# The last norm of a hybrid attention / recurrence layer: its weights ahead of the root, and several blocks of it in one product

## The chip, the cores and the metric

The kernel runs on one core of a Trainium2 chip. The metric is the device time of one execution, in microseconds (us). Engines: TensorE (PE), its weight loads (PEld), VectorE (DVE), ScalarE (ACT), GpSimd (POOL), and SyncE (SP), which only issues transfers; ScalarE issues some too.

## The reference, cut to what matters

One decoder layer on 1024 tokens of width 1024, all float32. After attention, recurrence and a gated MLP it ends in the MLP's down projection, the residual and a norm:

```python
h = h + conv_glu(u, w_up[layer], conv_w[layer], conv_b[layer], w_down[layer])
return rms_norm(h, final_norm_g)
# rms_norm(x, g) = x * rsqrt(mean(x * x, over the width) + 1e-6) * g
```

## The kernel before

All activations lie transposed: `h_` is a tile of 128 partitions x 8 blocks (`NCT`) x 1024 tokens, where block d holds 128 of the 1024 channels. A sum over the width is thus one over partitions and blocks: the squares of the eight blocks are added up, and a product with a matrix of ones on TensorE (`sum_parts`, L344, or L1377) brings the sum to all partitions.

Most of the down projection runs in seven stages (`STAGES`, L1417 and on; PE lines L1431 to L1433) and is added to `h_` at L1351. The rest, two of the 22 channel groups of the MLP, is done plainly by `down_piece(k, tail)` over `pieces`: piece 0 is tokens 0 to 511, piece 1 tokens 512 to 767, piece 2 tokens 768 to 1023. Pieces 1 and 2 are the end of the program, and the change is there.

- `down_block(d, t, name)`: six products on TensorE for one block (L1362 to L1364, tile `pdl`), and the residual addition on VectorE (L1365: one operand from PSUM, one from SBUF).
- `down_piece`: per block the addition above, a square on ScalarE (`sqf`, L1404; the first into an accumulator directly, `facc`, L1401), and the square's addition to an accumulator (L1405). Piece 1 has two accumulators, added at L1409, and the sum is split into a rounded part and the rest (`facchi` on ScalarE, L338; `facclo` on VectorE, L339) for the product with ones. Piece 2 has four, which go into four products with ones (L1377); its blocks 2 and 4 are added by GpSimd.
- `final(k)`: the product with ones (`ssf`), the root by Ln, Exp and Square on ScalarE (L328 to L330) and two steps on VectorE (`rft` L331, `rfy` L332), and then for each block one VectorE instruction that multiplies h by its weight and by the root (L1384), with a transfer to the output for each two blocks (L1389), or for each one of the last two (L1386).
- `down_piece(2, tail)` gets `final(1)` as `tail` and takes one step of it after each block from d = 4 on, so piece 1's root is worked out beside piece 2's blocks.

TensorE's instructions keep the order in which they are written. Those of the other engines are put in order by a scheduler when the program is built, except where `tc.keep_in_program_order` holds them: held instructions keep the written order among themselves on their engine.

Of the kernel before, what the change touches and what calls it, by code (L numbers as in the profile page):

```python
# [17 lines left out]
P = 128  # L18
SEQ = 1024
DM = 1024  # L20
# [182 lines left out]
def hybrid_kernel(ctx: ExitStack, tc: tile.TileContext, xT, w_qk, w_tok, w_hg, w_out, w_up,  # L203
# [1047 lines left out]
    with pool("ps2", "left", space=PSUM) as ps2:  # L1251
# [117 lines left out]
        facc = {}  # L1369

        def final(k):
            t = pieces[k]
            w = t.stop - t.start
            ss = bank2(f"ssf{k}")
            if k == 2:
                for i in range(4):
                    PE.matmul(ss[:, :w], ones, facc[k][i], start=(i == 0), stop=(i == 3))  # L1377
            else:
                sum_parts(ss[:, :w], facc[k])
            R, tt = (ttile(x, f"rf{x}_{k}", 2) for x in "yt")  # L1380
            rstd_part(R[:, :w], tt[:, :w], ss[:, :w], 1.0 / DM)
            yield
            for d in range(NCT):
                DVE.scalar_tensor_tensor(h_[:, d, t], h_[:, d, t], col(V_GF + d), R[:, :w], op0=ALU.mult, op1=ALU.mult)  # L1384
                if k == 2 and d >= 6:
                    (nc.sync if d % 2 else nc.scalar).dma_start(out[d, :, t], h_[:, d, t])  # L1386
                elif d % 2:
                    q = nc.scalar if k == 2 and d == 3 else nc.sync
                    q.dma_start(out[d - 1 : d + 1, :, t].rearrange("d p t -> p d t"), h_[:, d - 1 : d + 1, t])  # L1389
                yield  # L1390

        def down_piece(k, tail):
            t = pieces[k]
            w = t.stop - t.start
            facc[k] = [None] * 4
            for d in range(NCT):
                down_block(d, t, f"pdl{k}_{d}")
                i = d - 4 if d >= 6 and k == 2 else d % 2
                if facc[k][i] is None:
                    facc[k][i] = ttile(f"acc{i}", f"facc{k}_{i}", 2)[:, :w]  # L1400
                    ACT.activation(facc[k][i], h_[:, d, t], AF.Square)  # L1401
                else:
                    sq = ttile("sq", f"sqf{k}_{d}", 4)[:, :w]
                    ACT.activation(sq, h_[:, d, t], AF.Square)  # L1404
                    (POOL if k == 2 and d % 2 == 0 else DVE).tensor_add(facc[k][i], facc[k][i], sq)  # L1405
                if d >= 4:
                    next(tail, None)
            if k < 2:
                DVE.tensor_add(facc[k][0], facc[k][0], facc[k][1])  # L1409
                facc[k] = parts_of(facc[k][0], lambda x: ttile("sq", f"facc{x}{k}", 4, F32R)[:, :w])  # L1410
            for _ in tail:
                pass

        for x, y in STAGES:
            last = x == "s4"
            if last:
# [5 lines left out]

                down_piece(0, iter(()))
                tail = final(0)
# [36 lines left out]

        down_piece(1, tail)
        tail = final(1)
        down_piece(2, tail)
        for _ in final(2):
            pass
    tp_cm.__exit__(None, None, None)
    down_cm[0].__exit__(None, None, None)
# [64 lines left out]
```

## Time and profile before

| | us |
|---|---|
| median of 3 runs | 1209.05 (1207.75 to 1209.67) |
| the profiled execution | 1207.86 |
| its span, from the first instruction to the last | 1205.9 |
| outside the span | 1.96 |

Busy over the span: PE 1192.7 us (99%), DVE 947.8 (79%), ACT 631.4 (52%), POOL 298.5 (25%). By stretch of the span: from 1183.3 to 1189.0 (piece 1's products) DVE is busy 4.80 of 5.70 us and POOL not at all; from 1189.0 to 1195.4 (piece 2's) DVE 5.62 of 6.40, POOL 1.48; from 1195.4 to 1202.8 DVE 7.29 of 7.40, PE 1.31. Times in the text are microseconds from the start of the span; a bare four-digit time is a point on that clock.

### The profile page before, as it was taken

What the parts mean: (1) busy time and instruction counts of PE and PEld (TensorE: products, weight loads), DVE (VectorE), ACT (ScalarE), POOL (GpSimd) and SP (SyncE); (2) the same over time, 40 slices, a digit from 0 to 9 for tenths busy, and PEclk for the clock granted to TensorE, in tenths of its full rate; (3) what the DMA queues carried; (4) which work ended last, traced back from release to release, by engine and by line L of the source; (5) the groups of instructions that cost most, each with busy time, mean ns of one, the idle gap of its engine ahead of it and who ended that gap; (6) DMA issues with size and microseconds to landing.
All of it is one profiled execution on the core that took longest, in us unless ns stands there. A gap on an engine that the chain in (4) does not pass through costs nothing.

```text
span 1205.9 us, 17474 instructions
## 1 busy us (share of the span) xinstructions
PE 1192.7 (99%) x6014; PEld 1005.6 (83%) x6014; DVE 947.8 (79%) x1783; ACT 631.4 (52%) x1217; POOL 298.5 (25%) x276
## 2 busy tenths in 40 slices
PE   9999999999999999999999999999999999999996
PEld 8988888888888888888888888888888888888886
DVE  8767776666778776484999899898888978957986
ACT  8766666667666565454643343433443444444553
POOL 1154446544001014413231322312223200000000
PEclk9999999999999999999999999999999999999999
DMA  7021112223111123432113323333223267534532
GB/s 273 10 71 54 53 54 88 64 65 120 36 36 54 60 64 112 133 125 94 42 64 114 108 85 106 121 116 109 84 98 122 96 213 249 156 98 158 166 103 89
DMA packets 71833, 122.39 MB, mean 101 GB/s; under 512 B 7360, under 2 KB 17856, under 8 KB 71744
## 3 DMA queue, kind: packets, MB, share of 16 engines
q1 hardware_dynamic: 60528, 101.41, 26.3%
q10 hardware_dynamic: 11216, 19.86, 4.3%
q8 instruction: 47, 0.77, 0.3%
q14 instruction: 42, 0.34, 0.1%
HBM read 97.65 MB, written 23.59 MB: 101 GB/s over the span
## 4 chain that ended last, share of the span: by engine, by line
PE 95%; DVE 3%; ACT 1%; issue 0%; POOL 0%; DVEq 0%; ACTq 0%
PE p L1132 11%; PE p L1133 11%; PE p L1134 11%; PE ds L1433 3%; PE ds L1431 3%; PE ds L1432 3%; PE po L1036 2%; PE po L1038 2%; PE po L1037 2%; PE da L1433 2%; PE da L1431 2%; PE da L1432 2%; PE piv L512 1%; PE piv L514 1%; PE piv L513 1%; PE S L585 1%
## 5 line engine op out<-in xcount | busy, mean ns | idle before, releaser
L88 POOL TENSOR_TENSOR wlo<-raww,whi 128x512 fp32r<-128x512 f32 x141 | 208.6, 1491 | 382.4 <-ACT whi L86 231.6
L86 ACT CAST whi<-raww 128x512 fp32r<-128x512 f32 x276 | 167.7, 617 | 183.9 <-DVE raww L120 69.1
L88 DVE TENSOR_TENSOR wlo<-raww,whi 128x512 fp32r<-128x512 f32 x136 | 97.5, 717 | 22.8 <-ACT whi L86 22.7
L86 ACT CAST whi<-r 128x512 fp32r<-128x512 f32 x70 | 43.6, 623 | 83.1 <-PE ds L1432 51.3
L597 POOL TENSOR_SCALAR P<-P,st 128x512 f32<-128x512 f32 (+2 forms) x96 | 55.8, 592 | 107.9 <-DVE st L594 50.5
L588 DVE CUSTOM_DVE_ANT_0 P<-S,mask 128x512 f32<-128x512 f32 (+2 forms) x96 | 52.0, 553 | 29.9 <-PE S L586 28.9
L593 ACT ACTIVATE P<-P,st 128x128 f32<-128x128 f32 (+3 forms) x64 | 49.7, 777 | 32.0 <-DVE st L588 16.7
L88 DVE TENSOR_TENSOR wlo<-r,whi 128x512 fp32r<-128x512 f32 x70 | 47.9, 685 | 20.0 <-ACT whi L86 19.9
L624 DVE TENSOR_TENSOR tl<-T,th 128x512 fp32r<-128x512 f32 (+1 forms) x80 | 50.8, 634 | 16.2 <-ACT th L623 15.1
L1433 PE MATMUL ds<-fhi,wlo 128*128 128x512 f32 x160 | 62.3, 389 | 0.0
L1432 PE MATMUL ds<-flo,whi 128*128 128x512 f32 x160 | 62.3, 389 | 0.0
L1431 PE MATMUL ds<-fhi,whi 128*128 128x512 f32 x160 | 62.2, 389 | 0.0
L1132 PE MATMUL p<-b1h,whi 128*128 128x512 f32 x160 | 62.2, 389 | 0.0
L1133 PE MATMUL p<-b1l,whi 128*128 128x512 f32 x160 | 62.2, 389 | 0.0
L1134 PE MATMUL p<-b1h,wlo 128*128 128x512 f32 x160 | 62.2, 389 | 0.0
L1161 ACT ACTIVATE cv<-cv 128x512 f32<-128x512 f32 x44 | 27.9, 633 | 61.5 <-DVE cv L1154 61.4
L1154 DVE SCALAR_TENSOR_TENSOR cv<-g,vec,cv 128x511 f32<-128x511 f32 (+2 forms) x92 | 56.1, 615 | 4.7 <-ACT cv L1151 3.7
L1405 POOL TENSOR_TENSOR facc<-facc,sqf 128x256 f32<-128x256 f32 x2 | 1.5, 738 | 223.7 <-ACT sqf L1404 223.7
L623 ACT CAST th<-T 128x512 fp32r<-128x512 f32 (+1 forms) x80 | 43.0, 537 | 23.4 <-PE T L616 20.3
L86 ACT CAST fhi<-rawf 128x512 fp32r<-128x512 f32 x70 | 43.2, 617 | 15.2 <-DMA rawf<-spT 7.0
L88 DVE TENSOR_TENSOR flo<-rawf,fhi 128x512 fp32r<-128x512 f32 x70 | 47.9, 684 | 3.6 <-ACT fhi L86 3.6
L1431 PE MATMUL da<-fhi,whi 128*128 128x512 f32 x120 | 46.7, 389 | 0.0
(672 smaller groups left out, 3832.5 us busy)
## 6 DMA issues: line engine op xcount, KB each, us to landing
raww<-in_w_up_dram SPq DMA_DIRECT2D x88, 256.0 KB, 3.1
raww<-in_w_tok_dram SPq DMA_DIRECT2D x52, 256.0 KB, 2.7
rawf<-spT SPq DMA_DIRECT2D x40, 256.0 KB, 2.7
r<-in_w_down_dram SPq DMA_DIRECT2D x40, 256.0 KB, 3.5
raww<-in_w_hg_dram SPq DMA_DIRECT2D x32, 256.0 KB, 2.6
raww<-in_w_out_dram SPq DMA_DIRECT2D x32, 256.0 KB, 2.6
spB<-a ACTq DMA_DIRECT2D x30, 256.0 KB, 2.2
spT<-t ACTq DMA_DIRECT2D x30, 256.0 KB, 2.0
```

Of the source, the lines that this page charges most:

```text
L86: self.pin(self.high(hi[:, :w], raw))
L88: self.pin(low.tensor_sub(lo[:, :w], raw, f32(hi[:, :w])))
L588: DVE.tensor_tensor_reduce(Pt[:, k0 : k0 + w], S[:, :w], mask[:, m : m + w], -1.0, BIG * 3, op0=ALU.add, op1=ALU.min, accum_out=st[:, k0 / ...
L597: POOL.tensor_scalar(e, e, st[:, 3:4], 1.0, op0=ALU.mult, op1=ALU.mult)
L624: DVE.tensor_sub(tl[:, :n], T[:, :n], f32(th[:, :n]))
L1132: PE.matmul(ps, hi[:, s], bhi, start=(start and n == 0), stop=False)
L1133: PE.matmul(ps, hi[:, s], blo, start=False, stop=False)
L1134: PE.matmul(ps, lo[:, s], bhi, start=False, stop=(stop and n == len(rhs) - 1))
L1154: DVE.scalar_tensor_tensor(dst, x, col(V_CW + j * NFF + f), dst, op0=ALU.mult, op1=ALU.add)
L1431: PE.matmul(ps[d], hi[:, s], ahi, start=(k == 0), stop=False)
L1432: PE.matmul(ps[d], hi[:, s], alo, start=False, stop=False)
L1433: PE.matmul(ps[d], lo[:, s], ahi, start=False, stop=(k == NPAIR - 1))
```

## The change

In pieces 1 and 2 the norm's weight no longer goes into the same VectorE instruction as the root. Each block of h is multiplied by its weight first, in place, once its square has been taken: by GpSimd for piece 1's eight blocks and piece 2's blocks 0 to 2, by ScalarE for piece 2's blocks 3 to 7. The multiplication by the root (`scale`) is then a plain product of several blocks with one root tile, which is repeated by a step of zero: four blocks of piece 1, two more, and at the very end, among piece 2's four products of two blocks each, piece 1's last two. The transfers go with them: one of 512 KB and six of 256 KB; ScalarE's queue issues piece 2's blocks 0 and 1, its blocks 4 and 5, and piece 1's last two, and SyncE's the others, the very last one among them. Nearly all steps of the two pieces are held in the written order, on GpSimd too, and piece 1's sum is now written into piece 2's blocks step by step (`total`, `root`). GpSimd's two additions of piece 2 are the same as before; TensorE's instructions and their order are the same; piece 0 is the same.

```diff
-        def down_block(d, t, name):
+        def down_block(d, t, name, order=lambda ins: ins):
...
-            DVE.tensor_add(h_[:, d, t], ps[:, :w], h_[:, d, t])
+            order(DVE.tensor_add(h_[:, d, t], ps[:, :w], h_[:, d, t]))
...
+        def root(k):
...
+            order(ACT.activation(tt, ss, AF.Ln, bias=epst, scale=1.0 / DM))
+            yield y
+            order(ACT.activation(y, tt, AF.Exp, scale=-0.5))
+            order(ACT.activation(tt, y, AF.Square))
+            yield y
+            order(DVE.scalar_tensor_tensor(tt, ss, EPS * DM, tt, op0=ALU.add, op1=ALU.mult))
+            yield y
+            order(DVE.scalar_tensor_tensor(y, tt, -3.0 * DM, y, op0=ALU.add, op1=ALU.mult))
+            yield y
+
+        def gain(k, d, engine):
+            x = h_[:, d, pieces[k]]
+            if engine is ACT:
+                order(ACT.mul(x, x, col(V_GF + d)))
+            else:
+                order(POOL.tensor_scalar(x, x, col(V_GF + d), 1.0, op0=ALU.mult, op1=ALU.mult))
+
+        def scale(k, d, n, R, queue):
+            t = pieces[k]
+            x = h_[:, d : d + n, t]
+            order(DVE.tensor_mul(x, x, R.unsqueeze(1).to_broadcast([P, n, t.stop - t.start])))
+            queue.dma_start(out[d : d + n, :, t].rearrange("d p t -> p d t"), x)
...
+        def total(k):
+            order(DVE.tensor_add(facc[k][0], facc[k][0], facc[k][1]))
+            yield
...
+            order(ACT.copy(hi, facc[k][0]))
+            yield
+            order(DVE.tensor_sub(lo, facc[k][0], f32(hi)))
...
+            if k == 2:
+                before, chain = total(1), root(1)
+                next(before)
             for d in range(NCT):
-                down_block(d, t, f"pdl{k}_{d}")
+                down_block(d, t, f"pdl{k}_{d}", hold)
...
-                    (POOL if k == 2 and d % 2 == 0 else DVE).tensor_add(facc[k][i], facc[k][i], sq)
+                    hold(ACT.activation(sq, h_[:, d, t], AF.Square))
+                    if k == 2 and d % 2 == 0:
+                        order(POOL.tensor_add(facc[k][i], facc[k][i], sq))
+                    else:
+                        DVE.tensor_add(facc[k][i], facc[k][i], sq)
+                if k == 1:
+                    gain(1, d, POOL)
...
+        R = next(root1)
+        for d in (3, 4):
+            gain(2, d, ACT)
+        for d in range(3):
+            gain(2, d, POOL)
+        root2 = root(2)
+        next(root2)
+        next(root2)
+        for d in range(5, NCT):
+            gain(2, d, ACT)
+        scale(1, 0, 4, R, nc.sync)
+        scale(1, 4, 2, R, nc.sync)
+        next(root2)
+        R2 = next(root2)
+        for d in range(0, NCT, 2):
+            if d == 6:
+                scale(1, 6, 2, R, nc.scalar)
+            scale(2, d, 2, R2, nc.sync if d % 4 else nc.scalar)
```

What this makes of the order is seen at three places. First VectorE, where piece 1 ends and piece 2 begins. `pdl1_7` is the product of piece 1's block 7, `pdl2_0` that of piece 2's block 0, `sqf1_6` the square of piece 1's block 6, and `facc1_0`, `facc1_1` are piece 1's accumulators. Before:

```order
L1365 TENSOR_TENSOR h_5359<-pdl1_7_12019,h_5359 128x256
L1405 TENSOR_TENSOR facc1_0_11952<-facc1_0_11952,sqf1_6_12016 128x256
L1365 TENSOR_TENSOR h_5359<-pdl2_0_12035,h_5359 128x256
L1405 TENSOR_TENSOR facc1_1_11962<-facc1_1_11962,sqf1_7_12027 128x256
L1365 TENSOR_TENSOR h_5359<-pdl2_1_12045,h_5359 128x256
L1409 TENSOR_TENSOR facc1_0_11952<-facc1_0_11952,facc1_1_11962 128x256
L1365 TENSOR_TENSOR h_5359<-pdl2_2_12055,h_5359 128x256
L339 TENSOR_TENSOR facclo1_12032<-facc1_0_11952,facchi1_12031 128x256
```

Now, from the same place on to piece 2's block 7:

```order
L1365 TENSOR_TENSOR h_5359<-pdl1_7_12026,h_5359 128x256
L1460 TENSOR_TENSOR facc1_0_11952<-facc1_0_11952,sqf1_6_12022 128x256
L1460 TENSOR_TENSOR facc1_1_11963<-facc1_1_11963,sqf1_7_12034 128x256
L1425 TENSOR_TENSOR facc1_0_11952<-facc1_0_11952,facc1_1_11963 128x256
L1365 TENSOR_TENSOR h_5359<-pdl2_0_12039,h_5359 128x256
L1365 TENSOR_TENSOR h_5359<-pdl2_1_12052,h_5359 128x256
L1430 TENSOR_TENSOR facclo1_12050<-facc1_0_11952,facchi1_12049 128x256
L1365 TENSOR_TENSOR h_5359<-pdl2_2_12063,h_5359 128x256
L1365 TENSOR_TENSOR h_5359<-pdl2_3_12074,h_5359 128x256
L1460 TENSOR_TENSOR facc2_1_12061<-facc2_1_12061,sqf2_3_12082 128x256
L1365 TENSOR_TENSOR h_5359<-pdl2_4_12085,h_5359 128x256
```

Piece 1's last addition and its sum stood between piece 2's first residual additions; now both stand ahead of the first. Piece 2's residual addition of block 4 now stands behind the addition of block 3's square; it stood ahead of it.

Second VectorE from piece 2's block 5 to the end. Before:

```order
L1365 TENSOR_TENSOR h_5359<-pdl2_5_12098,h_5359 128x256
L1365 TENSOR_TENSOR h_5359<-pdl2_6_12110,h_5359 128x256
L331 SCALAR_TENSOR_TENSOR rft_1_12092<-ssf1_12088,rft_1_12092 128x256
L1405 TENSOR_TENSOR facc2_1_12053<-facc2_1_12053,sqf2_5_12106 128x256
L332 SCALAR_TENSOR_TENSOR rfy_1_12091<-rft_1_12092,rfy_1_12091 128x256
L1365 TENSOR_TENSOR h_5359<-pdl2_7_12122,h_5359 128x256
L1384 SCALAR_TENSOR_TENSOR h_5359<-h_5359,vec_63,rfy_1_12091 128x256 x8
L331 SCALAR_TENSOR_TENSOR rft_2_12147<-ssf2_12141,rft_2_12147 128x256
L332 SCALAR_TENSOR_TENSOR rfy_2_12146<-rft_2_12147,rfy_2_12146 128x256
L1384 SCALAR_TENSOR_TENSOR h_5359<-h_5359,vec_63,rfy_2_12146 128x256 x8
```

Now:

```order
L1365 TENSOR_TENSOR h_5359<-pdl2_5_12104,h_5359 128x256
L1460 TENSOR_TENSOR facc2_1_12061<-facc2_1_12061,sqf2_5_12112 128x256
L1365 TENSOR_TENSOR h_5359<-pdl2_6_12115,h_5359 128x256
L1389 SCALAR_TENSOR_TENSOR rft_1_12097<-ssf1_12093,rft_1_12097 128x256
L1365 TENSOR_TENSOR h_5359<-pdl2_7_12126,h_5359 128x256
L1391 SCALAR_TENSOR_TENSOR rfy_1_12096<-rft_1_12097,rfy_1_12096 128x256
L1406 TENSOR_TENSOR h_5359<-h_5359,rfy_1_12096 128x4x256
L1406 TENSOR_TENSOR h_5359<-h_5359,rfy_1_12096 128x2x256
L1389 SCALAR_TENSOR_TENSOR rft_2_12148<-ssf2_12142,rft_2_12148 128x256
L1391 SCALAR_TENSOR_TENSOR rfy_2_12147<-rft_2_12148,rfy_2_12147 128x256
L1406 TENSOR_TENSOR h_5359<-h_5359,rfy_2_12147 128x2x256 x3
L1406 TENSOR_TENSOR h_5359<-h_5359,rfy_1_12096 128x2x256
```

One more product of two blocks, piece 2's last, stands behind these. Sixteen products have become seven, of four blocks or of two; the addition of block 5's square has moved ahead of the residual additions of blocks 6 and 7.

Third GpSimd's end, as a piece of the difference:

```order
-L1405 TENSOR_TENSOR facc_0_12043<-facc_0_12043,sqf_2_12063 128x256
-L1405 TENSOR_TENSOR facc_0_12043<-facc_0_12043,sqf_4_12085 128x256
+L1400 TENSOR_SCALAR h<-h,vec 128x256 x8
+L1458 TENSOR_TENSOR facc_0_12047<-facc_0_12047,sqf_2_12071 128x256
+L1458 TENSOR_TENSOR facc_0_12047<-facc_0_12047,sqf_4_12099 128x256
+L1400 TENSOR_SCALAR h<-h,vec 128x256 x3
```

Its two additions now stand behind eight weight steps of piece 1 and ahead of three of piece 2. On ScalarE the order of squares, Ln, Exp and Square stays, but for `facchi`, which moves ahead of the square of piece 2's block 1; two weight steps stand ahead of piece 2's Ln and three behind its Square.

## Rows read from the trace of the kernel before

**Rows 1.** The page: the span, busy time of two engines (share of the span, instructions), and the shares of the chain that ended last by engine.

```profile
span 1205.9 us, 17474 instructions
...
PE 1192.7 (99%) x6014; PEld 1005.6 (83%) x6014; DVE 947.8 (79%) x1783; ACT 631.4 (52%) x1217; POOL 298.5 (25%) x276
...
PE 95%; DVE 3%; ACT 1%; issue 0%; POOL 0%; DVEq 0%; ACTq 0%
```

**Rows 2.** TensorE's timeline (start us, us, engine, line, operation, out<-in, shapes): the last product of piece 2's block 0, the last of its block 7, and the products with ones (two records each).

```profile
1188.75 0.28 PE L1364 MATMUL pdl<-ahi,w 128*128 128x256 f32 x1
...
1194.01 0.28 PE L1364 MATMUL pdl<-ahi,w 128*128 128x256 f32 x1
1194.17 2.55 PE L1377 MATMUL ssf<-facc,ones 128*128 128x256 f32 x8
```

**Rows 3.** The chain of waits from 1194 us to the end (start us, us, what).

```profile
1194.84 0.34 DVE rfy L332
1195.18 0.33 DVE h L1365
1195.51 3.16 DVE h L1384 x8
1198.68 0.35 DVE rft L331
...
1199.05 0.44 DVE rfy L332
...
1199.51 0.48 DVE h L1384
...
1200.39 2.37 DVE h L1384 x6
```

**Rows 4.** ScalarE's timeline: a square of piece 1, the sum's rounded part, and all from piece 2's square of block 3 to the second root's Square, without those of blocks 5 and 6 (in brackets the idle time before, and what ended it).

```profile
1185.21 0.42 ACT L1404 ACTIVATE sqf<-h 128x256 f32<-128x256 f32 x1 [0.30 <-DVE h L1365]
...
1190.63 0.41 ACT L338 CAST facchi<-facc 128x256 fp32r<-128x256 f32 x1
1191.03 0.42 ACT L1404 ACTIVATE sqf<-h 128x256 f32<-128x256 f32 x1
...
1192.54 0.46 ACT L328 ACTIVATE rft<-ssf,eps 128x256 f32<-128x256 f32 x1
1192.89 0.41 ACT L1404 ACTIVATE sqf<-h 128x256 f32<-128x256 f32 x1
1193.20 0.41 ACT L329 ACTIVATE rfy<-rft 128x256 f32<-128x256 f32 x1
1193.64 0.42 ACT L330 ACTIVATE rft<-rfy 128x256 f32<-128x256 f32 x1
...
1195.55 0.42 ACT L1401 ACTIVATE facc<-h 128x256 f32<-128x256 f32 x1 [0.88 <-DVE h L1365]
1196.75 0.47 ACT L328 ACTIVATE rft<-ssf,eps 128x256 f32<-128x256 f32 x1 [0.79 <-PE ssf L1377]
...
1197.70 0.42 ACT L330 ACTIVATE rft<-rfy 128x256 f32<-128x256 f32 x1
```

**Rows 5.** VectorE's timeline, from piece 1's block 3 and then at the change from piece 1 to piece 2 (x2 in the last row: residual additions of blocks 3 and 4).

```profile
1185.47 0.42 DVE L1365 TENSOR_TENSOR h<-pdl,h 128x256 f32<-128x256 f32 x1 [0.29 <-PE pdl L1364]
1185.81 0.41 DVE L1405 TENSOR_TENSOR facc<-facc,sqf 128x256 f32<-128x256 f32 x1
1186.19 0.43 DVE L1365 TENSOR_TENSOR h<-pdl,h 128x256 f32<-128x256 f32 x1
1186.53 0.41 DVE L1405 TENSOR_TENSOR facc<-facc,sqf 128x256 f32<-128x256 f32 x1
1186.91 0.42 DVE L1365 TENSOR_TENSOR h<-pdl,h 128x256 f32<-128x256 f32 x1
...
1189.07 0.42 DVE L1365 TENSOR_TENSOR h<-pdl,h 128x256 f32<-128x256 f32 x1
...
1191.08 0.43 DVE L339 TENSOR_TENSOR facclo<-facc,facchi 128x256 fp32r<-128x256 f32 x1
1191.42 0.96 DVE L1365 TENSOR_TENSOR h<-pdl,h 128x256 f32<-128x256 f32 x2
```

**Rows 6.** GpSimd's groups by shape (busy us, mean ns | idle before, releasers), and in the last row its first addition of piece 2 in the timeline.

```profile
L597 POOL TENSOR_SCALAR P<-P,st 128x256 f32<-128x256 f32 x16 | 7.7, 482 | 2.0 <-DVE st L594 2.0
...
L1405 POOL TENSOR_TENSOR facc<-facc,sqf 128x256 f32<-128x256 f32 x2 | 1.5, 738 | 223.7 <-ACT sqf L1404 223.7
...
1191.53 0.74 POOL L1405 TENSOR_TENSOR facc<-facc,sqf 128x256 f32<-128x256 f32 x1 [222.54 <-ACT sqf L1404]
```

**Rows 7.** Two places earlier in the kernel where VectorE and GpSimd overlap, in the timeline of either: a weight-like step on GpSimd and a VectorE addition of one column; and two additions on GpSimd, the second of which ends at 746.05, and a VectorE subtraction of 512 columns whose operands both lie in SBUF.

```profile
60.23 0.70 POOL L597 TENSOR_SCALAR P<-P,st 128x512 f32<-128x512 f32 x1
...
60.50 0.43 DVE L592 TENSOR_TENSOR st<-st 128x1 f32<-128x1 f32 x1
...
743.07 2.98 POOL L88 TENSOR_TENSOR wlo<-raww,whi 128x512 fp32r<-128x512 f32 x2 [2.07 <-ACT whi L86]
...
744.94 1.67 DVE L116 TENSOR_TENSOR raww<-raww,raww 128x512 f32<-128x512 f32 x1
```

**Rows 8.** VectorE's groups by shape: an element-wise instruction of 256 and of 512 columns, the products before, and one (the last row, from its line's own view: minimum, median, maximum ns) whose second operand is 128x4, repeated by a step of zero.

```profile
L1405 DVE TENSOR_TENSOR facc<-facc,sqf 128x256 f32<-128x256 f32 x8 | 3.3, 416 | 0.3 <-ACT sqf L1404 0.3
...
L88 DVE TENSOR_TENSOR wlo<-r,whi 128x512 fp32r<-128x512 f32 x70 | 47.9, 685 | 20.0 <-ACT whi L86 19.9
...
L1384 DVE SCALAR_TENSOR_TENSOR h<-h,vec,rfy 128x256 f32<-128x256 f32 x16 | 6.5, 478 | 0.0
...
L933 DVE TENSOR_TENSOR on<-psO,hss x8: 678/691/692, 351.1 to 496.7; 128x512 f32<-128x512 f32 x8
```

**Rows 9.** Transfers from 1199 to 1203 us (GB/s in 40 slices of 0.1 us; then issues by engine, KB each, median us from issue to landing), and the last issue in SyncE's timeline.

```profile
GB/s 389 389 379 389 389 154 184 399 389 369 399 389 358 134 10 0 0 0 0 0 0 0 0 205 410 369 389 410 358 348 134 102 369 369 369 410 379 369 236 195
...
out_dram<-h SPq DMA_DIRECT2D x3, 256.0 KB, 2.1
...
out_dram<-h SPq DMA_DIRECT2D x1, 128.0 KB, 2.0
...
1202.79 0.34 SPq L1386 DMA_DIRECT2D out_dram<-h  x1
```

More of the change, by code (lines that the diff above doesn't have):

```diff
@@ L1374, in final @@
             ss = bank2(f"ssf{k}")
[L1375 to L1379, printed above, removed]
+            sum_parts(ss[:, :w], facc[k])
             R, tt = (ttile(x, f"rf{x}_{k}", 2) for x in "yt")
@@ L1395, in down_piece @@
             facc[k] = [None] * 4
+            hold = order if k == 2 else lambda ins: ins
+            if k == 2:
+                before, chain = total(1), root(1)
+                next(before)
             for d in range(NCT):
-                down_block(d, t, f"pdl{k}_{d}")
+                down_block(d, t, f"pdl{k}_{d}", hold)
+                if k == 2 and d == 1:
+                    next(before)
+                elif k == 2 and d == 4:
+                    next(chain)
+                elif k == 2 and d == 6:
+                    next(chain)
                 i = d - 4 if d >= 6 and k == 2 else d % 2
@@ L1400, in down_piece @@
                     facc[k][i] = ttile(f"acc{i}", f"facc{k}_{i}", 2)[:, :w]
-                    ACT.activation(facc[k][i], h_[:, d, t], AF.Square)
+                    hold(ACT.activation(facc[k][i], h_[:, d, t], AF.Square))
                 else:
                     sq = ttile("sq", f"sqf{k}_{d}", 4)[:, :w]
-                    ACT.activation(sq, h_[:, d, t], AF.Square)
-                    (POOL if k == 2 and d % 2 == 0 else DVE).tensor_add(facc[k][i], facc[k][i], sq)
-                if d >= 4:
-                    next(tail, None)
-            if k < 2:
+                    hold(ACT.activation(sq, h_[:, d, t], AF.Square))
+                    if k == 2 and d % 2 == 0:
+                        order(POOL.tensor_add(facc[k][i], facc[k][i], sq))
+                    else:
+                        DVE.tensor_add(facc[k][i], facc[k][i], sq)
+                if k == 1:
+                    gain(1, d, POOL)
+                if k == 2 and d == 0:
+                    next(before)
+                elif k == 2 and d == 4:
+                    next(chain)
+            if k == 2:
+                return chain
+            if k == 0:
                 DVE.tensor_add(facc[k][0], facc[k][0], facc[k][1])
                 facc[k] = parts_of(facc[k][0], lambda x: ttile("sq", f"facc{x}{k}", 4, F32R)[:, :w])
-            for _ in tail:
-                pass
         for x, y in STAGES:
@@ L1421, in ttile @@
                     return otile(tags[tag][0], name, tags[tag][1], dt)
-                down_piece(0, iter(()))
+                down_piece(0)
                 tail = final(0)
@@ L1460, in ttile @@
             return tp.tile([P, H2], dt, tag=tag, name=name, bufs=bufs)
[L1462 to L1465, printed above, removed]
-            pass
+        down_piece(1)
+        for _ in tail:
+            pass
+        root1 = down_piece(2)
+        R = next(root1)
[16 more added lines that the diff above has]
+            scale(2, d, 2, R2, nc.sync if d % 4 else nc.scalar)
     tp_cm.__exit__(None, None, None)
```

20 lines of the change are left out of this document (14 added, 6 removed).

## Prediction, made before the changed kernel was run

> **What bounds the kernel now.** First the page: TensorE is busy 1192.7 of 1205.9 us and holds 95% of the chain that ends last [rows 1], so work beside it is free until its last product. TensorE's timeline then says where that is: the last product of piece 2 ends at 1194.29, and only products with ones follow, to 1196.72 [rows 2]. The change lives in the 11.6 us after 1194.29 and in what it delays before. Next the chain of waits: from 1194.84 it stands on VectorE, eight products of piece 1 (3.16 us), the two steps of piece 2's root, eight products again, which end at 1202.76 [rows 3]. That looks like an engine that is full, and seven products for sixteen look like a gain. But ScalarE's timeline shows the root's Square done at 1198.12 [rows 4], and VectorE takes it up at 1198.60 [rows 3]: without any product in the way, the second root would start 0.45 us earlier and no more. Behind VectorE there is a second chain, square, sum, Ln, Exp, Square, nearly as long, and the change reorders what feeds it.
>
> **The change, part by part.** I walk the new order with durations and handovers of the rows. A dependent instruction starts some 0.04 us after its operand (`facchi` ends 1191.04, `facclo` starts 1191.08) [rows 4, 5], GpSimd 0.08 after a square (1191.45 to 1191.53) [rows 4, 6]; independent ones follow on VectorE 0.08, on ScalarE 0.1 before the end of the one ahead [rows 4, 5].
>
> *Weights on GpSimd in piece 1.* Nobody waits for them soon, yet they are not free. The nearest row for their time is the same instruction in the same shape, 0.482 us [rows 6]. A one-column addition on VectorE that began at 60.50, during such a step, lasted 0.43 and ended at 60.93, with the step; a subtraction of 512 columns from SBUF began under a GpSimd addition that ended at 746.05 and ended at 746.61, 0.56 later [rows 7]. So a VectorE instruction with both operands in SBUF that starts during a GpSimd step finishes its columns after it: GpSimd's end plus 0.28 for 256 columns. Block 2's square ends at 1185.63, its weight step runs from 1185.71 to 1186.19, and VectorE starts that square's addition at 1185.81 [rows 4, 5]: it ends at 1186.47, not 1186.22. VectorE has no slack to absorb it: residual addition plus square's addition take 0.72, TensorE's pace [rows 5]. By this step block 7's residual addition ends at 1189.17, 0.40 late, and the additions of squares 6 and 7 and the sum, again under weight steps, end at 1189.81, 1190.14 and 1190.78.
>
> *The sum ahead of piece 2's first residual addition.* That one started at 1189.07, 0.04 after its product [rows 2, 5]; behind the sum it ends at 1191.12, not 1189.49. Its square starts at 1191.16, `facchi` 0.32 behind it, `facclo` ends at 1192.34 instead of 1191.51 [rows 5]: **+0.83**. TensorE's ones-product waits for it, so its last block ends about 1194.95; that costs nothing as VectorE comes later still. Residual additions 2 and 3 follow, the second ending at 1193.03.
>
> *Block 4 behind block 3's square.* That square ends at 1193.54. GpSimd's own addition (0.738 [rows 6]), released by block 2's square, runs 1193.22 to 1193.96, so VectorE's ends at 1194.24, and the residual addition of block 4, now behind it, at 1194.58; it ended at 1192.38 [rows 5]: **+2.2**.
>
> *ScalarE's queue.* Exp stands behind block 4's square, as before (1192.89, 1193.20 [rows 4]). That square now ends at 1195.09; Exp, Square and block 5's square follow, to 1196.18. VectorE's order now wants that square's addition ahead of residual additions 6 and 7, so it idles from 1194.92 to 1196.22. Then 6, a root step and 7, which ends at 1197.67; it ended at 1195.51 [rows 3]: **+2.16**.
>
> *The second root.* Its last square ends 0.45 later, TensorE needs 0.74 more (1195.97 to 1196.72 [rows 2, 4]), and from there to the end of Square are 1.42 (1196.75 to 1198.12 plus handover [rows 4]): Square ends at 1200.28, not 1198.12. Two weight steps on ScalarE run while TensorE sums; they cost nothing as long as the sum takes longer. Meanwhile VectorE's products of piece 1 (four blocks, two blocks) are over by 1199.8. So the root's steps start at 1200.31 instead of 1198.60: the shorter products give back 0.45 of the 2.16, **+1.71**.
>
> *Merged products.* 256 columns take 0.416, 512 take 0.685 [rows 8], so 0.27 per 256 columns and some 0.08 saved between neighbours; an operand repeated by a step of zero costs nothing extra (0.691 for 512 [rows 8]). Five products of two blocks after the root: four at 0.60 and the last 0.68, 3.08, against 3.25 for eight (1199.51 to 1202.76 [rows 3]): **-0.17**. They end at 1204.30 instead of 1202.76, **+1.54**. Weight steps of piece 2 (three on GpSimd from 1195.9, three on ScalarE from 1200.2) are over at 1197.5 and 1201.2, ahead of their products.
>
> *Transfers.* The last one is 256 KB, not 128: median to landing 2.1 for 2.0 [rows 9]. Five of 256 KB come 0.60 apart, and the transfer engines move at most some 387 GB/s [rows 9], 0.68 per 256 KB: the fifth waits 4 x 0.08. Together **+0.38**, between 0.07 (no backlog) and 0.45.
>
> Sum: 1.54 + 0.38 = **+1.92 us**. Against the profiled execution (1207.86) that is 1209.8. Its time lies 1.19 under the median of the runs shown, so against that median I forecast **1211.0**.
>
> One page bears on the largest unknown. The Trainium skill, SBUF — State Buffer, section "SBUF: two separate sides", has VectorE (with two SBUF inputs) and GpSimd share a port pair that is locked for a whole instruction, the other fully blocked. The trace agrees that the later one waits, but the one-column addition ended with GpSimd's step: its fixed part had already run [rows 7]. By the page taken to the letter, the held instruction would run in full afterwards, and the sum would be that of the second rival below.
>
> Unknowns kept for the range: the hold-up per addition, from nothing (first rival) to a full restart (second); the weight step's time, 0.482 to the 0.738 of GpSimd's addition [rows 6], which would be slower than a block's 0.72, add 1.4 and reach 1212.4; handovers, some twenty on the path, each good for 0.02.
>
> **The rivals.** (1) GpSimd's steps do not hold VectorE up; order alone acts. For it: the hold-up by such a step is read from one instruction of one column, the other from a two-operand addition [rows 7]. The same walk without hold-ups ends the products at 1203.45: +0.69, with transfers +1.07, **1210.1**. (2) On the other side of 0.2%: a held addition starts anew after GpSimd's step, so each pays 0.42 instead of 0.28. Every addition of piece 1's squares, and two of piece 2's, then end 0.14 to 0.3 later, and the walk ends at 1205.22: +2.46, with transfers +2.84, **1211.9**. It decides once the path loses 0.5 more than forecast, which is three or four such additions. Against it: the 60.93 of [rows 7]. (3) The order costs nothing: ScalarE's and VectorE's waits close up, the Square comes at 1198.12 as before, and the products gain in full: -0.45 - 0.17 + 0.38 = -0.24, **1208.8**. Against it: the addition of block 5's square waits behind Exp and Square on ScalarE, whatever else is early. (4) The change does not do what it says. The order shows its products merged and its weights ahead; only the two additions named as VectorE's are no move against this kernel, since GpSimd has two before and two after. A wait on a transfer that is hidden would leave 1209.05.
>
> **How the numbers follow.** Chances: forecast 0.51, (1) 0.18, (2) 0.19, (3) 0.10, (4) 0.02. A measurement of this kernel can tell about 0.2%, 2.4 us, from no change; the runs shown spread by 1.9. The forecast's +1.92 has some 0.7 to either side, so about a fifth of it lies over 2.4; of (2) three quarters do. Slower by over 0.2%: 0.10 + 0.15 + a little of (1), 0.27. Faster by over 0.2% has no mechanism, since the best case is -0.6 without transfers; 0.03 for the runs' spread. The rest, 0.70, is no change that can be told, on the slow side of it. The range runs from just under (3), 1208.6, to 1212.8, past (2) and the slow weight steps.
>
> **What would show it.** In the changed profile: weight steps of about 0.48 on GpSimd in piece 1; additions of squares of 0.6 to 0.7 instead of 0.416 beside them; `facclo` near 1192.3; VectorE idle for over a microsecond before the addition of block 5's square, put down to ScalarE; the second Square near 1200.3 and the root taken up at once, with no product in its way; last products of 0.68 that end near 1204.3; the last landing 2.4 after its issue. The prediction is wrong if VectorE has no idle time there, if the additions keep 0.416, or if the second root still waits for products.

## The result, and the profile after

| kernel | median us | kernel before beside it | ratio, 95% interval | span | tail starts | tail |
|---|---|---|---|---|---|---|
| before | | | | 1205.9 | 1183.31 | 22.60 |
| changed | 1210.47 | 1208.58 | 1.0014 [1.0008, 1.0020] | 1209.7 | 1185.11 | 24.54 |
| e_after_again (changed) | 1210.66 | 1208.62 | 1.0013 [1.0004, 1.0021] | 1208.8 | 1184.30 | 24.55 |
| e_no_w1 | 1209.62 | 1208.37 | 1.0011 [1.0002, 1.0020] | 1207.8 | 1183.81 | 24.01 |
| e_sum_late | 1209.37 | 1208.37 | 1.0009 [1.0000, 1.0018] | 1207.5 | 1183.85 | 23.65 |
| e_sq3_late | 1209.18 | 1208.37 | 1.0006 [0.9998, 1.0015] | 1207.6 | 1183.91 | 23.64 |
| e_s1_early | 1209.64 | 1208.37 | 1.0012 [1.0003, 1.0021] | 1208.0 | 1183.95 | 24.00 |
| e_sq5_late | 1209.87 | 1208.30 | 1.0015 [1.0006, 1.0024] | 1207.7 | 1183.27 | 24.42 |
| e_exp_late | 1209.34 | 1208.30 | 1.0009 [1.0000, 1.0018] | 1207.8 | 1183.94 | 23.88 |
| e_w1_alone (on before) | 1208.38 | 1208.30 | 1.0000 [0.9991, 1.0009] | 1206.1 | 1183.67 | 22.46 |
| e_w1_stt (on before) | 1209.49 | 1208.62 | 1.0005 [0.9996, 1.0014] | 1206.9 | 1184.03 | 22.89 |
| e_best | 1207.53 | 1208.30 | 0.9993 [0.9984, 1.0001] | 1205.9 | 1183.99 | 21.89 |
| e_best_single | 1208.04 | 1208.62 | 0.9995 [0.9986, 1.0004] | 1205.3 | 1183.32 | 21.95 |
| e_best_no_w1 | 1207.18 | 1208.62 | 0.9989 [0.9980, 0.9997] | 1206.6 | 1185.07 | 21.49 |

The changed kernel is 1.89 us slower, 0.14%: less than the 0.2% that the prediction took as the least that can be told, though the interval of the ratio excludes 1: with 21 runs of either kernel a smaller difference can be told than it assumed. The forecast was +1.92 on a median of 1209.05; with more runs the kernel before has 1208.58, so 1210.47 lies 0.5 under the 1211.0.

Times differ here by 1 us, and a run scatters by as much. So most of what follows is read in the **tail**: from the start of piece 1's first residual addition to the end of the span. Code ahead of that point is the same in all kernels, yet it was reached between 1183.27 and 1185.11, so a span says little. The tails of the changed kernel's two profiles differ by 0.01. Differences in the text are taken from the traces in nanoseconds; they can lie 0.01 off those of the figures shown. To lay a point of the changed profile beside one of before, subtract 1185.11 - 1183.31 = 1.80.

The page of the changed kernel, as [rows 1], with GpSimd's weight steps:

```profile
span 1209.7 us, 17479 instructions
...
PE 1194.7 (99%) x6014; PEld 1005.9 (83%) x6014; DVE 948.3 (78%) x1774; ACT 633.5 (52%) x1222; POOL 303.3 (25%) x287
...
PE 90%; DVE 6%; ACT 2%; issue 1%; POOL 0%; DVEq 0%; ACTq 0%
...
L1400 POOL TENSOR_SCALAR h<-h,vec 128x256 f32<-128x256 f32 x11 | 5.8, 535 | 217.2 <-ACT facc L1453 215.5
```

VectorE has as much to do as before. What changed is the chain: TensorE held 95% of it, now 90%.

VectorE's timeline of the changed kernel, as [rows 5], on to the second root and the last products, which [rows 3] shows as parts of the chain:

```profile
1185.11 0.42 DVE L1365 TENSOR_TENSOR h<-pdl,h 128x256 f32<-128x256 f32 x1
...
1187.62 0.66 DVE L1460 TENSOR_TENSOR facc<-facc,sqf 128x256 f32<-128x256 f32 x1
...
1190.88 0.41 DVE L1460 TENSOR_TENSOR facc<-facc,sqf 128x256 f32<-128x256 f32 x1
1191.51 0.43 DVE L1460 TENSOR_TENSOR facc<-facc,sqf 128x256 f32<-128x256 f32 x1 [0.21 <-ACT sqf L1456]
1191.97 0.58 DVE L1425 TENSOR_TENSOR facc<-facc,facc 128x256 f32<-128x256 f32 x1
1192.47 0.74 DVE L1365 TENSOR_TENSOR h<-pdl,h 128x256 f32<-128x256 f32 x2
1193.66 0.42 DVE L1430 TENSOR_TENSOR facclo<-facc,facchi 128x256 fp32r<-128x256 f32 x1 [0.45 <-ACT facchi L1428]
...
1195.30 0.74 DVE L1460 TENSOR_TENSOR facc<-facc,sqf 128x256 f32<-128x256 f32 x1 [0.54 <-ACT sqf L1456]
...
1197.97 0.50 DVE L1460 TENSOR_TENSOR facc<-facc,sqf 128x256 f32<-128x256 f32 x1 [1.27 <-ACT sqf L1456]
1198.39 0.41 DVE L1365 TENSOR_TENSOR h<-pdl,h 128x256 f32<-128x256 f32 x1
...
1202.11 0.42 DVE L1389 SCALAR_TENSOR_TENSOR rft<-ssf,rft 128x256 f32<-128x256 f32 x1 [0.38 <-ACT rft L1387]
...
1203.10 3.10 DVE L1406 TENSOR_TENSOR h<-h,rfy 128x512 f32<-128x512 f32 x5
```

GpSimd's timeline beside it, as [rows 6]:

```profile
1187.52 0.48 POOL L1400 TENSOR_SCALAR h<-h,vec 128x256 f32<-128x256 f32 x1 [0.24 <-ACT sqf L1456]
...
1190.84 1.44 POOL L1400 TENSOR_SCALAR h<-h,vec 128x256 f32<-128x256 f32 x2 [0.49 <-ACT sqf L1456]
1195.02 0.74 POOL L1458 TENSOR_TENSOR facc<-facc,sqf 128x256 f32<-128x256 f32 x1 [2.74 <-ACT sqf L1456]
...
1197.72 1.55 POOL L1400 TENSOR_SCALAR h<-h,vec 128x256 f32<-128x256 f32 x3
```

Read the two together. The addition at 1187.62 began 0.09 after a weight step and ended at 1188.27, 0.27 after that step's end at 1188.00. The addition at 1195.30 began under GpSimd's own addition, which ended at 1195.75, and ended at 1196.03, 0.28 later. Before, the first took 0.41 [rows 5] and the second 0.43. The residual addition at 1198.39, with one operand in PSUM, also began under a weight step (1198.17 to 1198.81), took 0.41 and was not held.

The chain of waits where it turns from VectorE to ScalarE and back, as [rows 3] (start us, us, what):

```profile
1191.97 0.58 DVE facc L1425
1192.55 0.34 DVE h L1365
...
1195.30 0.74 DVE facc L1460
1196.03 0.35 DVE h L1365
...
1196.46 0.42 ACT sqf L1456
1196.88 0.32 ACT rfy L1386
...
1197.21 0.42 ACT rft L1387
1197.63 0.32 ACT sqf L1456
...
1197.97 0.50 DVE facc L1460
```

This is the order in one view: piece 1's sum ahead of piece 2's first residual addition, then held addition, residual addition of block 4, square 4, Exp, Square, square 5, and only then the addition that VectorE stood 1.27 us for. In [rows 3] the chain is on VectorE from 1194.84 to the last product, and no row of ScalarE stands in it any more.

The transfers, as [rows 9] (GB/s in 40 slices of 0.165 us from 1203.0, then the last issue alone):

```profile
GB/s 391 391 385 391 379 385 317 25 0 0 106 379 391 379 360 391 385 391 385 391 366 391 385 373 391 391 391 360 391 385 385 180 0 0 0 0 0 0 0 0
...
out_dram<-h SPq DMA_DIRECT2D x1, 256.0 KB, 2.4
```

From 1204.7 the line of five transfers runs without a gap at some 387 GB/s.

### The profile page after: what moved, and what is told of

Its sections match the earlier page's. It is cut to its first block, busy times and chain, and to the rows that moved or that the text cites. A ratio compares the mean times of both kernels' runs of the same rounds, so it can differ in the third digit from the quotient of the medians.

```text
span 1209.7 us, 17479 instructions
## 1 busy us (share of the span) xinstructions
PE 1194.7 (99%) x6014; PEld 1005.9 (83%) x6014; DVE 948.3 (78%) x1774; ACT 633.5 (52%) x1222; POOL 303.3 (25%) x287
## 4 chain that ended last, share of the span: by engine, by line
PE 90%; DVE 6%; ACT 2%; issue 1%; POOL 0%; DVEq 0%; ACTq 0%
PE p L1134 10%; PE p L1133 10%; PE p L1132 10%; PE ds L1490 3%; PE ds L1492 3%; PE ds L1491 3%; PE po L1036 2%; PE po L1038 2%; PE po L1037 2%; PE da L1490 2%; PE da L1491 2%; PE da L1492 2%; PE piv L512 1%; PE piv L514 1%; PE piv L513 1%; PE S L585 1%
## 5 line engine op out<-in xcount | busy, mean ns | idle before, releaser
L624 DVE TENSOR_TENSOR tl<-T,th 128x512 fp32r<-128x512 f32 (+1 forms) x80 | 50.7, 634 | 16.2 <-ACT th L623 15.1
L1400 POOL TENSOR_SCALAR h<-h,vec 128x256 f32<-128x256 f32 x11 | 5.8, 535 | 217.2 <-ACT facc L1453 215.5
```

The source lines that it names most:

```text
L624: DVE.tensor_sub(tl[:, :n], T[:, :n], f32(th[:, :n]))
```

## The experiments

Each edit is made to the changed kernel unless it says otherwise.

**e_no_w1: what the hold-ups cost.**

```diff
-                if k == 1:
-                    gain(1, d, POOL)
```

> The changed kernel without GpSimd's eight weight steps of piece 1 (so this piece of the output lacks its weight vector); order untouched. Tail = from the start of piece 1's first residual addition to the end of the span: 24.6 us in the changed kernel, 22.6 before. Theory (a weight step holds the addition that starts under it until its own end plus the columns): additions of piece 1's squares fall from 0.47-0.66 to 0.41-0.43 us, the sum from 0.58 to 0.43, block 7's residual addition ends 0.40 earlier counted from the tail's start, facclo 0.6 earlier; GpSimd's own addition still holds square 3's addition, so the whole chain behind shifts by the same 0.6: tail 24.0, 0.6 us faster than the changed kernel. Rival 'order alone acts' (the hold-ups are absorbed by waits behind them): tail 24.6, no difference. Rival 'a held addition starts anew': 0.9 or more back, tail 23.7 or less.

Tail 24.01, **0.53 less** than the changed kernel. VectorE's timeline, first addition of a square and the sum:

```profile
1186.31 0.41 DVE L1460 TENSOR_TENSOR facc<-facc,sqf 128x256 f32<-128x256 f32 x1
...
1190.28 0.42 DVE L1425 TENSOR_TENSOR facc<-facc,facc 128x256 f32<-128x256 f32 x1
```

The additions of piece 1's squares are back at 0.41 to 0.43, and the 0.54 by which `facclo` comes earlier reaches the end whole. Neither rival fits: not absorbed, not 0.9.

**e_sum_late: the sum's place.**

```diff
                 before, chain = total(1), root(1)
-                next(before)
...
-                if k == 2 and d == 1:
+                if k == 2 and d in (0, 2):
                     next(before)
```

> The changed kernel with piece 1's sum behind piece 2's first residual addition and facclo behind its third, as the kernel before had it; all else as changed. Theory (the sum ahead of that addition starts the whole late chain): residual addition 0 of piece 2 ends 0.64 earlier in the tail, facclo 0.5 earlier, block 3's square and GpSimd's addition 0.6 to 1.1 earlier, residual addition 4 1.1 earlier, and as every later step hangs on it, the tail falls by 1.1, from 24.6 to 23.5. Rival 'the hold on square 3's addition and Exp's place decide by themselves': the tail falls by 0.5 at most (facclo's share, through Ln and Exp). Rival 'order costs nothing': 24.6.

Tail 23.65, **0.89 less**. VectorE's timeline, piece 2's first residual addition, the sum, and square 3's addition:

```profile
1190.58 0.42 DVE L1365 TENSOR_TENSOR h<-pdl,h 128x256 f32<-128x256 f32 x1
1190.92 0.42 DVE L1425 TENSOR_TENSOR facc<-facc,facc 128x256 f32<-128x256 f32 x1
...
1193.49 0.43 DVE L1459 TENSOR_TENSOR facc<-facc,sqf 128x256 f32<-128x256 f32 x1 [0.82 <-ACT sqf L1455]
```

Square 2 comes 1.15 earlier, GpSimd's addition with it, and it no longer meets VectorE's: 0.43 instead of 0.74. Square 3 comes only 0.54 earlier, hence 0.9, not 1.1: it starts 0.37 after its residual addition is done, and what else it waits for the profile does not name.

**e_sq3_late: square 3's addition behind residual addition 4.**

```diff
+                if k == 2 and d == 4:
+                    order(DVE.tensor_add(held[0], held[0], held[1]))
...
+                    elif k == 2 and d == 3:
+                        held = facc[k][i], sq
                     else:
```

> The changed kernel with VectorE's addition of square 3 in piece 2 one place later, behind residual addition 4; all else as changed. Theory (residual addition 4 stands behind an addition that GpSimd holds; square 4, Exp, Square and square 5 queue behind it on ScalarE): residual addition 4 ends 1.2 earlier, Exp then waits for its Ln instead of square 4, square 5 ends 0.87 earlier, VectorE's idle stretch before its addition stays over 0.7, tail 23.7, 0.87 faster than the changed kernel. Rival 'ScalarE's Ln is the limit, not the residual': tail 24.3 or more. Rival 'order costs nothing': 24.6.

Tail 23.64, **0.90 less**. VectorE's timeline, residual additions 2 to 4 in one row, then the held addition and the later one:

```profile
1192.81 1.08 DVE L1365 TENSOR_TENSOR h<-pdl,h 128x256 f32<-128x256 f32 x3
1194.10 0.74 DVE L1445 TENSOR_TENSOR facc<-facc,sqf 128x256 f32<-128x256 f32 x1 [0.21 <-ACT sqf L1458]
...
1195.85 0.52 DVE L1464 TENSOR_TENSOR facc<-facc,sqf 128x256 f32<-128x256 f32 x1 [0.68 <-ACT sqf L1458]
```

The addition is held as long as before (0.74), but now nobody stands behind it. Residual addition 4 ends 1.28 earlier; 0.9 of it arrives, because square 4 then stands behind Ln on ScalarE.

**e_exp_late: Exp and Square behind square 5.**

```diff
-                elif k == 2 and d == 6:
+                elif k == 2 and d == 7:
                     next(chain)
...
-                elif k == 2 and d == 4:
+                elif k == 2 and d == 5:
                     next(chain)
```

> The changed kernel with Exp and Square of piece 1's root behind block 5's square on ScalarE, and the root's first step on VectorE behind residual addition 7; all else as changed. Theory (Exp and Square, 0.75 us of ScalarE with the pitch, delay the square that VectorE's order waits for): square 5 ends 0.75 earlier, residual addition 7 0.8 earlier, Exp and Square now stand ahead of squares 6 and 7 but have room there, tail 23.9, 0.6 faster than the changed kernel. Rival 'piece 1's root is what the end waits for': it comes later, tail 24.5 or more. Rival 'order costs nothing': 24.5.

Tail 23.88, **0.66 less**: square 5 ended 0.75 earlier in the tail, and Square of piece 1's root, 0.31 later than in the changed kernel, held nobody up: the root's first step stands behind residual addition 7 by the same edit. ScalarE's squares 4 and 5, and VectorE's addition of square 5:

```profile
1195.29 0.72 ACT L1456 ACTIVATE sqf<-h 128x256 f32<-128x256 f32 x2 [0.81 <-DVE h L1365]
...
1196.04 0.81 DVE L1460 TENSOR_TENSOR facc<-facc,sqf 128x256 f32<-128x256 f32 x1 [0.52 <-ACT sqf L1456]
```

So the edit does not move ScalarE's queue alone. The addition now begins under GpSimd's addition of square 4 and is held (0.81 instead of 0.50), which takes 0.31 back; the root's first step, no longer ahead of residual addition 7, gives 0.33. The two cancel, and residual addition 7 ends 0.77 earlier. The last 0.1 is lost between the last square and Ln (0.89, not 0.79).

**e_sq5_late: fill the idle stretch.**

```diff
+                if k == 2 and d == 7:
+                    order(DVE.tensor_add(held[0], held[0], held[1]))
...
+                    elif k == 2 and d == 5:
+                        held = facc[k][i], sq
                     else:
```

> The changed kernel with VectorE's addition of square 5 in piece 2 behind residual addition 7, so that VectorE no longer stands idle (1.27 us) for that square; all else as changed. Theory (the idle stretch is a symptom: squares 5, 6, 7 stand in ScalarE's queue and the addition cannot be earlier than square 5): residual addition 7 ends 1.0 earlier in the tail, yet the addition itself now ends at 13.7-13.8 after the tail's start instead of 13.36, and three products with ones on TensorE stand behind it, so the sum's end and the tail stay: 24.5, within 0.15. Rival 'VectorE's idle stretch is the loss': root and products come 1.0 earlier, tail 23.5.

Tail 24.42, **0.12 less**, within 0.15 as expected. VectorE's timeline from residual additions 4 to 6 on:

```profile
1194.12 1.07 DVE L1365 TENSOR_TENSOR h<-pdl,h 128x256 f32<-128x256 f32 x3
1195.82 0.42 DVE L1389 SCALAR_TENSOR_TENSOR rft<-ssf,rft 128x256 f32<-128x256 f32 x1 [0.63 <-ACT rft L1387]
...
1196.50 0.58 DVE L1451 TENSOR_TENSOR facc<-facc,sqf 128x256 f32<-128x256 f32 x1
...
1200.14 0.42 DVE L1389 SCALAR_TENSOR_TENSOR rft<-ssf,rft 128x256 f32<-128x256 f32 x1 [0.79 <-ACT rft L1387]
```

VectorE's longest idle stretch in the tail was worth a tenth of itself: it moved to the second root (0.79). Behind the addition, which ends at 1197.08, Ln starts 1.66 later; in the changed kernel it starts 0.79 after the last square. Between lie three products with ones on TensorE instead of one, in the order in which they are written; that order was not tried.

**e_s1_early: piece 1's last product ahead of the second root.**

```diff
         scale(1, 4, 2, R, nc.sync)
+        scale(1, 6, 2, R, nc.scalar)
         next(root2)
...
-            if d == 6:
-                scale(1, 6, 2, R, nc.scalar)
```

> The changed kernel with piece 1's last product (two blocks) and its transfer ahead of piece 2's root instead of between its products; all else as changed. Theory (VectorE is idle for 0.38 before the second root's first step, since that waits for ScalarE's Square): the product fills the gap, the root's steps start 0.05 to 0.2 later, one product of 0.60 less stands behind it, one transfer of 256 KB less stands in the line at the end: last product 0.5 earlier, tail 24.0. Rival 'VectorE is full there' (the root is pushed by the whole product): products end as now, tail 24.6; it would be 24.5 by the shorter line of transfers alone.

Tail 24.00, **0.54 less**. VectorE's timeline, three products, the root's first step, four products:

```profile
1198.76 2.43 DVE L1406 TENSOR_TENSOR h<-h,rfy 128x1024 f32<-128x1024 f32 x3
1201.11 0.42 DVE L1389 SCALAR_TENSOR_TENSOR rft<-ssf,rft 128x256 f32<-128x256 f32 x1
...
1202.09 2.50 DVE L1406 TENSOR_TENSOR h<-h,rfy 128x512 f32<-128x512 f32 x4
```

The root started 0.16 later in the tail, and a product of 0.60 was gone behind it, so the last product ended 0.45 earlier; the other 0.10 is the line of transfers, shorter by one (last landing 2.37 after the last product, not 2.46). VectorE was not full there.

**e_w1_alone and e_w1_stt, on the kernel before: GpSimd's weight steps in the old order.** The first with plain products for piece 1:

```diff
+                if k == 1:
+                    x = h_[:, d, t]
+                    tc.keep_in_program_order(
+                        POOL.tensor_scalar(x, x, col(V_GF + d), 1.0, op0=ALU.mult, op1=ALU.mult))
                 if d >= 4:
...
+                if k == 1:
+                    DVE.tensor_mul(h_[:, d, t], h_[:, d, t], R[:, :w])
...
```

> The kernel before with one part of the change alone: GpSimd's eight weight steps in piece 1 and plain products for that piece; order, single products and transfers as before. Theory (the hold-up costs by itself): the first held addition ends 0.25 later, block 7's residual addition 0.4 later, sum 0.7 later, residual addition 7 of piece 2 0.5 later, and as the second root is then no longer behind products alone, the tail goes from 22.6 to 23.1, 0.5 slower than before. Rival 'waits behind it absorb it in the old order': 22.6. Rival 'a held addition starts anew': 23.5 or more.

Tail 22.46, **0.14 less than before**: the expectation of +0.5 missed. The second Square did come later in the tail, by 0.29, so the old order does not absorb the hold-up either. But the eight products between the roots, in VectorE's timeline:

```profile
1196.07 2.77 DVE L1385 TENSOR_TENSOR h<-h,rfy 128x256 f32<-128x256 f32 x8
1198.80 0.42 DVE L331 SCALAR_TENSOR_TENSOR rft<-ssf,rft 128x256 f32<-128x256 f32 x1
```

take 2.77, not the 3.25 of eight with a weight [rows 3, 8], which I had assumed. A second theory then: a hold-up of 0.29 (not 0.5), hidden by a gain of 0.48 in products that the second root had to wait for. The second kernel adds the same weight steps (the first four added lines above) and keeps the products as they were:

> The kernel before with GpSimd's eight weight steps in piece 1 added and nothing else: VectorE's products of that piece keep their weight (so this piece of the output has the weight twice). Theory (the weight steps delay the second root by 0.29 as in the experiment with plain products, and the plain products, 0.34 apart instead of 0.40, hid it): Square 2 ends at 15.1 in the tail, the eight products end at 15.57, the second root's first step begins at 15.55, last product at 19.75, tail 22.85, 0.28 slower than before. Rival 'the old order absorbs the hold-up by itself': 22.57. Rival 'a held addition starts anew': 23.2 or more.

Tail 22.89, **0.29 more than before**; the same rows there:

```profile
1196.43 3.25 DVE L1384 SCALAR_TENSOR_TENSOR h<-h,vec,rfy 128x256 f32<-128x256 f32 x8
1199.60 0.42 DVE L331 SCALAR_TENSOR_TENSOR rft<-ssf,rft 128x256 f32<-128x256 f32 x1
```

The second Square ends at 15.10 in the tail and the last product at 19.74, as expected (15.1 and 19.75). The median's ratio (1.0005) is too wide to add anything.

**e_best: all parts of the change, another order.** The edits of e_sum_late, e_sq3_late and e_s1_early, and square 5's addition behind residual addition 6 and the root's first step. Up to the products that is nearly the order of the kernel before.

```diff
+                    elif k == 2 and d in (3, 5):
+                        held = facc[k][i], sq
...
                 elif k == 2 and d == 6:
                     next(chain)
+                    order(DVE.tensor_add(held[0], held[0], held[1]))
```

> The changed kernel in another order, with all its parts (weights ahead, merged products): piece 1's sum behind piece 2's first residual addition and facclo behind its third, square 3's addition behind residual addition 4, square 5's behind residual addition 6 and the root's first step, piece 1's last product ahead of piece 2's root. Theory (the loss is the order, the merged products are a gain that the order hides): residual addition 7 ends at about 12.1 in the tail as before, the second root's steps start at about 14.9 instead of 17.0 (before 15.3), last product at 18.4 (before 19.45), but the transfers then set the end at 387 GB/s for 1 MB: tail 21.9, 0.7 faster than the kernel before and 2.6 faster than the changed one. Rival 'GpSimd's weight steps cost in any order': 0.5 of that is lost, tail 22.4. Rival 'the transfers are at their limit before too': tail 22.6, as before.

Tail 21.89: **0.71 less than before, 2.65 less than the changed kernel**; by the medians 0.77 and some 2.7. VectorE's timeline, and the transfers (40 slices of 0.175 us from 1199.0):

```profile
1196.58 2.52 DVE L1406 TENSOR_TENSOR h<-h,rfy 128x1024 f32<-128x1024 f32 x3
1199.02 0.41 DVE L1389 SCALAR_TENSOR_TENSOR rft<-ssf,rft 128x256 f32<-128x256 f32 x1
...
1200.00 2.50 DVE L1406 TENSOR_TENSOR h<-h,rfy 128x512 f32<-128x512 f32 x4
```

```profile
GB/s 380 386 404 392 386 374 381 375 392 374 381 398 386 392 287 287 380 386 380 375 392 386 392 381 386 380 381 375 392 374 334 24 0 0 0 0 0 0 0 0
```

The root starts 0.25 earlier in the tail than before, the last product ends 0.94 earlier (2.50 for 3.25 us), and 0.31 of that goes to the line of transfers (what follows the last landing is 0.08 shorter), now almost unbroken from 1199.0 to 1204.4. The ratio's interval still touches 1; the tail and the rows show the gain, the medians alone do not.

**e_best_single: is it the merging?** e_best with piece 2's products one block at a time.

```diff
-            scale(2, d, 2, R2, nc.sync if d % 4 else nc.scalar)
...
+            for x in (h_[:, d, t], h_[:, d + 1, t]):
+                order(DVE.tensor_mul(x, x, R2))
...
```

> The reordered kernel (all parts of the change, other order) with piece 2's products taken one block at a time, eight for four; the transfers of two blocks stay. Theory (a product without weight costs VectorE 0.34 a block at the pitch, a merged one 0.60 for two, so merging is worth 0.08 a pair, and the line of transfers, 0.68 for 256 KB, sets the end): products end 0.25 to 0.3 later, the last landing only 0.07 to 0.15 later, tail 21.95. Rival 'merging is the gain': the tail grows by 0.19 a pair, 0.7, to 22.6.

Tail 21.95, **0.05 more** than e_best. Its products, in VectorE's timeline:

```profile
1199.32 2.77 DVE L1547 TENSOR_TENSOR h<-h,rfy 128x256 f32<-128x256 f32 x8
```

Of the 0.75 us that eight products save, 0.48 come from leaving the weight out and 0.27 from merging; the transfers hide nearly all of the latter.

**e_best_no_w1: is the hold-up gone there?** e_best with the edit of e_no_w1.

> The reordered kernel without GpSimd's eight weight steps of piece 1 (so this piece of the output lacks its weight vector). Theory (in this order too the hold-up of 0.29 stands on the path through the sum, Ln and ScalarE's queue): Square 2 ends 0.25 to 0.3 earlier, but VectorE's three products of piece 1 end only as much earlier as the first root does; tail 21.6. Rival 'the order absorbs it': 21.86, no difference. Rival 'a hold-up of 0.6 as in the changed order': 21.3.

Tail 21.49, **0.40 less**: more than the 0.29 expected, less than 0.53. VectorE's sum ends 0.39 earlier in the tail and every later step follows. The hold-up costs 0.3 to 0.5 in all three orders.

**e_after_again: the 1.8 us ahead of the tail.**

> The changed kernel once more, nothing edited, beside the others. In its first profile the tail (from piece 1's first residual addition to the end) took 24.5 us and began at 1185.11, 1.8 later than in the kernel before (1183.31); in the experiments with the same code ahead of the tail it began at 1183.27 to 1183.99. Theory (the 1.8 is scatter of one execution ahead of the edit): the tail begins between 1183.2 and 1184.2 and takes 24.5; median 1.9 above the kernel before. Rival 'the change delays what stands ahead of it too': the tail begins at 1185 again.

Tail 24.55; it starts at 1184.30, 0.1 past the range I gave but not at 1185 again, while e_best_no_w1, whose edit lies behind that point, starts at 1185.07. So the start scatters from one execution to the next. The traces show where. Beside the kernel before, TensorE's instructions lie between 0.05 us early and 0.77 late at 12 us, and most executions keep that within 0.2 up to the tail. In three, both of the changed kernel and e_best_no_w1, they fall another 1.1 behind at one place. TensorE's timeline of the changed kernel there:

```profile
615.28 0.50 PE L1134 MATMUL p<-b22h,wlo 128*128 128x512 f32 x1 [0.69 <-DVE wlo L88]
```

Why `wlo` comes late in these three and not in the others, no run here shows. That the changed kernel always loses this 1.1, and the kernel before never, does not fit the medians: they lie 1.89 and 2.04 over the kernel before, and its tail alone is 1.94 longer.

## Why the prediction was right, step by step

Points of the changed profile less 1.80, beside the forecast:

| step | forecast | measured |
|---|---|---|
| first held addition ends | 1186.47 | 1186.47 |
| block 7's residual addition ends | 1189.17 | 1189.16 |
| addition of square 6 ends | 1189.81 | 1189.49 |
| sum ends | 1190.78 | 1190.75 |
| `facclo` ends | 1192.34 | 1192.29 |
| residual addition of block 4 ends | 1194.58 | 1194.57 |
| square 5 ends | 1196.18 | 1196.14 |
| residual addition of block 7, piece 2, ends | 1197.67 | 1197.66 |
| second Square ends | 1200.28 | 1200.27 |
| second root's first step starts | 1200.31 | 1200.31 |
| last product ends | 1204.30 | 1204.39 |
| last landing less last product | 2.45 | 2.46 |

**Weights on GpSimd.** Right in size: a held addition pays its columns, not all of itself. The experiments put 0.53 of the loss on this step. One detail fell: at 1190.88 VectorE won, and GpSimd's step took 0.72 instead of 0.48. It cost nothing, since square 7 came later anyway. The next step was held by the addition at 1191.51 and took 0.71, to 1192.28; the sum's 0.58 is the wait for it.

The Trainium skill, SBUF — State Buffer, section "SBUF: two separate sides", says that the engine that starts first has the port pair for the whole instruction and the other is fully blocked. That somebody waits, the trace shows at each of these rows. But at 1190.88 the one whose record starts 0.04 later was not held, and a held one took 0.27 to 0.28 for 256 columns behind the other's end, not the 0.41 of a full run.

**The sum's place, block 4 behind square 3, ScalarE's queue.** Each is shown by an experiment: 0.89, 0.90, 0.66, the last with the root's first step moved too. They are one path, so these do not add up. The chain of waits named them all.

**The second root.** The prediction's 1198.60 for the start of this root before is not in [rows 3], where the chain counts it from the end of the product ahead, 1198.68; it is in VectorE's timeline of the kernel before:

```profile
1198.60 0.42 DVE L331 SCALAR_TENSOR_TENSOR rft<-ssf,rft 128x256 f32<-128x256 f32 x1
```

As forecast, nothing stands in its way now (0.03 after Square, 0.48 before), and the shorter products give back 0.44. e_s1_early shows that it left 0.38 unused.

**Merged products.** Five in 3.10 for eight in 3.25: -0.16, forecast -0.17. The term was right, its reason only in part: the weight left out does more than the merging. The handover ahead of them took 0.10, not 0.04. So the last product is +1.63, not +1.54.

**Transfers.** From the last product to the last landing +0.40, forecast +0.38; what follows the landing became 0.09 shorter, which the forecast had as unchanged. 1.63 + 0.40 - 0.09 = +1.94, the tails' difference. So the path is as forecast, but that the sum comes within 0.02 is partly luck: a last product 0.09 too late and an end 0.09 shorter cancel.

**The rivals.** (1), no hold-up, falls with e_no_w1; (2), a restart, with every held row; (3), an order that costs nothing, with e_sum_late, e_sq3_late and e_exp_late; (4), a change that does not do what it says, with the changed profile, which has GpSimd's eleven weight steps and the merged products. A neighbour of (3) is true all the same: in the order of e_best the parts of the change gain 0.7.

## What to carry to other kernels

Before you move work to GpSimd, look at which VectorE instructions with two SBUF operands will run beside it, and add their columns behind its end (0.27 to 0.28 us for 256 here). When an engine's order is fixed by hand, ask of each instruction what it may be held by and who queues behind it: a held addition costs little with nobody behind it, and 0.9 us ahead of the one instruction that feeds the next engine. An idle stretch is read from the wait at its end: filling it brought 0.1 us, moving what that wait stood for 0.7 to 0.9.

## What the runs showed of the hardware that was not expected

- Which of GpSimd and VectorE is held hangs on a few hundredths: a VectorE addition that started 0.04 us after a GpSimd step ran freely (0.41) and the step took 0.72; one that started 0.09 after it was held (0.66). GpSimd steps held in this way ended 0.26 (0.72) and 0.35 (0.71) after VectorE's end, the second by an addition that had begun 0.06 ahead of the step.
- Products of two 128x256 tensors follow each other at 0.34 us, with a per-partition scalar besides at 0.40: eight take 2.77 and 3.25.
- The output leaves at 380 to 390 GB/s whatever the grouping, so with 1 MB behind the last root, products faster than 0.68 us for 256 KB gain little: eight single products cost 0.05 more than four merged ones.
